# Two of four adaLN gate parts move from TensorE to VectorE in a one-core diffusion block

## The chip, the core and the metric

The kernel runs on one core of a Trainium2 chip. A core has TensorE (PE in the profile, with PEld for its weight loads), VectorE (DVE), ScalarE (ACT), GpSimd (POOL) and SyncE (SP), which here only issues DMAs. Each engine takes its instructions in the order in which they were written into its queue and waits on semaphores for the others. The metric is device time in microseconds: the median of several executions. One further execution was profiled, and all rows below are from it.

## What is computed

The reference is one layer of a diffusion block: 256 latent tokens and 256 context tokens of 2048 channels, all in fp32. The conditioning vector c gives six vectors of 2048 numbers through one matrix `w_ada`; the third of them, `g_a`, is the gate of the attention sub-layer, and it is first needed where the output projection is added to x.

```
sh_a, sc_a, g_a, sh_m, sc_m, g_m = ada_modulation(c, w_ada[layer], b_ada[layer])   # silu(c) @ w + b
h = modulate(rms_norm(x, norm_attn_w[layer]), sh_a, sc_a)
q, k, v, u = split_projection(h @ w_in[layer])
...
attn = latent_window_attention(q, k, v, kc, vc, attn_sink[layer])
pool = multiscale_pool(u, pool_w[layer], pool_scale[layer])
x = x + g_a * (jnp.concatenate([attn, pool], axis=-1) @ w_out[layer])
hm = modulate(rms_norm(x, norm_mlp_w[layer]), sh_m, sc_m)
x = x + g_m * squared_relu_mlp(hm, w_mlp_up[layer], w_mlp_down[layer])
```

## The kernel before

All weights stream through one ring. `WeightStream` holds a list of 1 MB tiles in the order of use and loads them with DMAs from the SP queue into five buffers named `raw` (`N_RAW`, L25). A load can start when the tile five places ahead in the list has been given back, and the SP queue issues the loads strictly in that order. A weight tile is split for the matmuls by ScalarE (`hi`, L97) and VectorE (`lo`, L98), and is given back after that. An adaLN tile (`in_w_ada`) is not split: it is given back when the engine that multiplies it with silu(c) has read it.

Each adaLN vector is cut into parts of 512 columns (`g` in ADA_LATE, the gate) or of 256 columns of shift and scale together (`m`). A part has four steps, one for each of its four tiles, and then a finish. There are two ways to do the steps. `ada_pe` (L292) lets TensorE multiply a step's tile with `c_sil` into `ps_ada`, four matmuls that the profile shows as eight instructions, and ScalarE copies the sum to `ada_e` after the fourth step (L311). `ada_dve` (L315) lets VectorE do it: one TENSOR_SCALAR (L325) and fifteen SCALAR_TENSOR_TENSOR (L327) for a part, four instructions for a step, each adding to the one before. In both cases a TensorE matmul over the partitions finishes the part: `ps_g` for the gate (L526), which VectorE adds to the gate tile `ga` (L528).

The list ADA_LATE (L32) fixes the order of the parts and the engine of each. `late_steps` (L514) goes through it; `run_late` (L537) does one step, and does the finish of the part before when the next part begins. During the attention 20 steps are placed: the part m1 and the four gate parts g0 to g3. The parts m2 to m4 come in the output projection (`LATE_OUT`).

The attention itself is 16 units (`Unit`, L706: eight pairs of heads by two blocks of queries). A unit is a chain over three engines: scores `ps_s` on TensorE (L717 to L720), maxima on VectorE (L728 to L730), exponentials on ScalarE (L736, L734), sum and reciprocal on VectorE (L740, L741), normalisation on ScalarE (L744), transposes `tp_p` on TensorE (L752), their copy `pT` on ScalarE (L754). After every second unit `attend` multiplies with the values (`ps_o`, L763), and ScalarE and VectorE split the result into `mx` (L766, L767). The pooling mixer (`ps_pool`) is woven in. Then comes the output projection (`ps_w`), which needs the weight tiles of `w_out`.

The order on each engine is not the written order: the kernel is built with a scheduler that lays out the program on a simulated timeline and writes each engine's queue from that. A change in one step so reorders its neighbours too. The gate parts are called part 0 to part 3 below (j in ADA_LATE).

Of the kernel before, what the change touches and what calls it, by code (L numbers as in the profile page):

```python
# [8 lines left out]
F32 = mybir.dt.float32  # L9
# [6 lines left out]
P = 128  # L16
# [14 lines left out]

ADA_LATE = (  # L32
    ("m", 0, "pe"), ("m", 1, "pe"),
    ("g", 0, "pe"), ("g", 1, "pe"), ("g", 2, "pe"), ("g", 3, "pe"),
    ("m", 2, "dve"), ("m", 3, "dve"), ("m", 4, "dve"), ("m", 5, "pe"), ("m", 6, "dve"), ("m", 7, "dve"),
)
LATE_IN = 4
# [87 lines left out]
def kernel(  # L125
# [10 lines left out]
    const = ctx.enter_context(tc.tile_pool(name="const", bufs=1, side="left"))  # L136
# [131 lines left out]
    def rstd(pool, ss, n, rest=EPS):  # L268

        nv = pool.tile([P, n], F32, tag="rs_v", name="rs_v", bufs=2)  # L270
        y = pool.tile([P, n], F32, tag="rs_y", name="rs_y", bufs=2)
        u = pool.tile([P, n], F32, tag="rs_u", name="rs_u", bufs=2)
        nc.vector.tensor_scalar(nv, ss, 1.0 / D, rest, ALU.mult, ALU.add)
        nc.vector.tensor_scalar(u.bitcast(I32), nv.bitcast(I32), 1, None, ALU.logical_shift_right)
        nc.vector.tensor_scalar(y.bitcast(I32), u.bitcast(I32), -1, 0x5F3759DF, ALU.mult, ALU.add)
        nc.vector.tensor_scalar(nv, nv, -0.5, None, ALU.mult)
        for _ in range(3):
            for c_ in range(n):
                yc, uc = y[:, c_ : c_ + 1], u[:, c_ : c_ + 1]
                nc.vector.scalar_tensor_tensor(uc, yc, nv[:, c_ : c_ + 1], yc, ALU.mult, ALU.mult)  # L280
            for c_ in range(n):
                yc, uc = y[:, c_ : c_ + 1], u[:, c_ : c_ + 1]
                nc.vector.scalar_tensor_tensor(yc, uc, 1.5, yc, ALU.add, ALU.mult)
        return y
# [30 lines left out]
    def ada_dve(finish):  # L315

        box = {}

        def step(kg):
            raw = S.next("ada")  # L320
            for j in range(4):
                sc = c_sil[:, 4 * kg + j, 0:1]
                if kg == 0 and j == 0:
                    box["e"] = mp.tile([P, 512], F32, tag="ada_v", name="ada_v", bufs=1)
                    nc.vector.tensor_scalar(box["e"], raw[:, j, :], sc, None, ALU.mult)  # L325
                else:
                    nc.vector.scalar_tensor_tensor(box["e"], raw[:, j, :], sc, box["e"], ALU.mult, ALU.add)  # L327

        return [lambda kg=kg: step(kg) for kg in range(4)] + [lambda: finish(box["e"])]

    def ada_cols(e, weights):

        ps = bank("ps_adac")
        for j in range(4):
            nc.tensor.matmul(ps[:, 2 * j : 2 * j + 2], e[:, 128 * j : 128 * j + 128], weights, start=True, stop=True)
        return ps[:, 0:8].rearrange("p (j s) -> p j s", s=2)
# [177 lines left out]
    def late_steps():  # L514
        for what, j, engine in ADA_LATE:
            ada, weights, spread = (ada_pe, sel, selb) if engine == "pe" else (ada_dve, ones[:, 0:2], ones)

            def finish(e, what=what, j=j, weights=weights, spread=spread):
                if what == "m":
                    k = slice(2 * j, 2 * j + 2)  # L520
                    ps = ada_cols(e, weights)
                    ada_scale(am[:, k], ps[:, 0:2], bcol[:, 64 + 2 * j : 66 + 2 * j], cols[:, 48 + 2 * j : 50 + 2 * j])
                    ada_shift(sm[:, k], ps[:, 2:4], bcol[:, 48 + 2 * j : 50 + 2 * j])
                else:
                    ps = bank("ps_g")
                    nc.tensor.matmul(ps, spread, e, start=True, stop=True)  # L526
                    gs = gate["a"][:, 512 * j : 512 * j + 512]
                    nc.vector.tensor_tensor(gs, ps, gs, ALU.add)  # L528

            steps = ada(finish)  # L530
            yield from steps[:4]
            late_finish.append(steps[4])
# [290 lines left out]
    mp = ctx.enter_context(tc.tile_pool(name="mp", bufs=1, side="right", reuse_waits="tile"))  # L823
# [150 lines left out]
    for b in range(7):  # L974
        acts = early[0:2] if b == 0 else [early[2], up_group()] if b == 1 else [up_group(), up_group()]
        steps = ada_dve(lambda e, b=b: gate_m_chunk(b, e)) if b < 4 else None
        for dg in range(4):
            pss = down_group(b, dg, acts)
            for i in range(2):
                accumulate(y[dg][:, i, :], pss[i], b == 0)  # L980
            if steps:
                steps[dg]()
                if dg == 3:
                    steps[4]()
# [29 lines left out]
    def finish(i, ts, last):  # L1014

        n = 3 + len(ts)
        nc.vector.tensor_reduce(mean[:, i : i + 1], ss3[:, i, 0:n], axis=AX.X, op=ALU.add)
        nc.vector.tensor_scalar(mean[:, i : i + 1], mean[:, i : i + 1], 1.0 / D, EPS, ALU.mult, ALU.add)
        ts.append(last())
        r = rstd(yp, ss3[:, i, n : n + 1], 1, mean[:, i : i + 1])  # L1020
        w = D - 1536
        for h, t in enumerate(ts):
            s = slice(1536 + w // len(ts) * h, 1536 + w // len(ts) * (h + 1))
            nc.vector.scalar_tensor_tensor(x2[:, i, s], t, r, fw[:, s], ALU.mult, ALU.mult)
        for q, eng in ((3, nc.sync), (0, nc.sync), (1, nc.scalar), (2, nc.sync)):
            xs = x2[:, i, 512 * q : 512 * q + 512]
            if q < 2 or q == 2 and i == 0:
                nc.scalar.activation(xs, xs, AF.Copy, scale=r)
            elif q == 2:
                nc.vector.tensor_scalar(xs, xs, r, None, ALU.mult)  # L1030
            eng.dma_start(out=out[P * i : P * i + P, 512 * q : 512 * q + 512], in_=xs)
# [70 lines left out]
```

## Time and profile before

| what | value |
|---|---|
| median of 3 runs | 1147.65 us (1146.72 to 1148.39) |
| the profiled execution | 1147.05 us, its span 1145.3 us |
| PE busy | 1104.6 us, 96% of the span |
| DVE busy | 779.2 us, 68% |
| ACT busy | 523.6 us, 46% |
| DMA | 286.66 MB, 250 GB/s on the mean |

The span is the profiled stretch; 1.75 us of the execution lie outside it. Busy shares are means over stages that differ: the input projection ends at about 205 us, the attention lies between about 205 and 306 us, the output projection between 306 and 402 us, and the MLP takes the rest. Matmuls overlap one another, and their ends are modelled, so a PE that is busy all the time is not at its peak.

### The profile page before, as it was taken

What the parts mean: (1) busy time and instruction counts of PE and PEld (TensorE: products, weight loads), DVE (VectorE), ACT (ScalarE), POOL (GpSimd) and SP (SyncE); (2) the same over time, 40 slices, a digit from 0 to 9 for tenths busy, and PEclk for the clock granted to TensorE, in tenths of its full rate; (3) what the DMA queues carried; (4) which work ended last, traced back from release to release, by engine and by line L of the source; (5) the groups of instructions that cost most, each with busy time, mean ns of one, the idle gap of its engine ahead of it and who ended that gap; (6) DMA issues with size and microseconds to landing.
All of it is one profiled execution on the core that took longest, in us unless ns stands there. A gap on an engine that the chain in (4) does not pass through costs nothing.

```text
span 1145.3 us, 16131 instructions
## 1 busy us (share of the span) xinstructions
PE 1104.6 (96%) x6364; PEld 909.3 (79%) x6364; DVE 779.2 (68%) x1222; ACT 523.6 (46%) x796; POOL 37.0 (3%) x53
## 2 busy tenths in 40 slices
PE   4999999999999989999999999999999999999996
PEld 2767778856588869888888888888888888888885
DVE  4655567875588988696774874884664565587576
ACT  4633233499734343365343443433444443443452
POOL 1000001610000000000000000000000000000000
PEclk9999999999999989899999999999999999999998
DMA  9999898687799989977775776775566556566532
GB/s 343 359 341 336 288 325 264 210 292 259 267 369 314 325 306 332 336 246 259 262 265 184 257 269 195 253 267 192 184 192 202 194 184 185 191 192 204 184 110 75
DMA packets 174013, 286.66 MB, mean 250 GB/s; under 512 B 5608, under 2 KB 72352, under 8 KB 172784
## 3 DMA queue, kind: packets, MB, share of 16 engines
q1 hardware_dynamic: 172800, 279.55, 72.9%
q0 software_dynamic: 848, 5.55, 1.3%
q8 instruction: 50, 0.82, 0.3%
q10 hardware_dynamic: 288, 0.52, 0.1%
q14 instruction: 27, 0.22, 0.1%
HBM read 283.50 MB, written 2.10 MB: 249 GB/s over the span
## 4 chain that ended last, share of the span: by engine, by line
PE 88%; DVE 4%; ACT 3%; DMA 3%; issue 1%; SPq 0%; ACTq 0%; DVEq 0%
PE ps_up L919 25%; PE ps_d L288 10%; PE ps_d L289 10%; PE ps_d L290 10%; PE ps_ada L305 4%; PE ps_w L288 3%; PE ps_w L290 3%; PE ps_w L289 3%; PE ps_qu L288 2%; PE ps_qu L290 2%; PE ps_qu L289 2%; PE ps_up L288 1%; DVE lo L98 1%; PE ps_o L763 1%; PE ps_up L289 1%; PE ps_up L290 1%
## 5 line engine op out<-in xcount | busy, mean ns | idle before, releaser
L98 DVE TENSOR_TENSOR lo<-raw,hi 128x1024 fp32r<-128x1024 f32 x330 | 397.7, 1226 | 211.8 <-ACT hi L97 201.0
L97 ACT CAST hi<-raw 128x1024 fp32r<-128x1024 f32 x330 | 338.1, 1050 | 409.1 <-PE ps_up L919 151.7
L919 PE MATMUL ps_up<-mx,hi 128*128 128x512 f32 x832 | 200.1, 393 | 0.0
L288 PE MATMUL ps_d<-hi,ahi 128*128 128x512 f32 (+1 forms) x520 | 200.0, 386 | 0.0
L289 PE MATMUL ps_d<-lo,ahi 128*128 128x512 f32 (+1 forms) x520 | 200.0, 386 | 0.0
L290 PE MATMUL ps_d<-hi,alo 128*128 128x512 f32 (+1 forms) x520 | 198.7, 386 | 0.0
L919 PEld LDWEIGHTS ps_up<-mx,hi 128*128 128x128 f32 x832 | 153.4, 188 | 31.8 <-issue 1.9
L290 PEld LDWEIGHTS ps_d<-hi,alo 128*128 128x128 f32 x520 | 97.7, 188 | 19.8
L288 PEld LDWEIGHTS ps_d<-hi,ahi 128*128 128x128 f32 x520 | 97.7, 188 | 19.5
L289 PEld LDWEIGHTS ps_d<-lo,ahi 128*128 128x128 f32 x520 | 97.7, 188 | 19.3
L919 PEld LDWEIGHTS ps_up<-mx,lo 128*128 128x128 f32 x832 | 106.7, 191 | 4.0
L327 DVE SCALAR_TENSOR_TENSOR ada_v<-raw,c_sil,ada_v 128x512 f32<-128x512 f32 x135 | 100.9, 748 | 12.7 <-DMA raw<-in_w_ada_dram 11.1
L919 PE MATMUL ps_up<-mx,lo 128*128 128x256 f32 x832 | 107.9, 283 | 0.0
L288 PE MATMUL ps_qu<-hhi,hi 128*128 128x256 f32 x240 | 69.3, 290 | 1.4 <-ACT hi L97 1.4
L305 PE MATMUL ps_ada<-raw,c_sil 128*32 128x512 f32 x480 | 68.3, 628 | 2.2 <-DMA raw<-in_w_ada_dram 1.9
L290 PE MATMUL ps_qu<-hhi,lo 128*128 128x256 f32 x240 | 67.0, 282 | 0.3 <-DVE lo L98 0.3
L289 PE MATMUL ps_qu<-hlo,hi 128*128 128x256 f32 x240 | 66.9, 280 | 0.0
L288 PEld LDWEIGHTS ps_qu<-hhi,hi 128*128 128x128 f32 x240 | 45.1, 188 | 16.6 <-issue 8.4
L288 PE MATMUL ps_up<-mx,hi 128*128 128x256 f32 x192 | 54.7, 293 | 1.8 <-ACT mx L884 1.5
L289 PE MATMUL ps_up<-mx,hi 128*128 128x256 f32 x192 | 54.3, 287 | 0.0
L290 PE MATMUL ps_up<-mx,lo 128*128 128x256 f32 x192 | 53.1, 287 | 0.4 <-DVE lo L98 0.4
L288 PE MATMUL ps_w<-hi,mx 128*128 128x512 f32 x128 | 50.4, 395 | 0.0
(202 smaller groups left out, 1336.4 us busy)
## 6 DMA issues: line engine op xcount, KB each, us to landing
raw<-in_w_ada_dram SPq DMA_DIRECT2D x128, 512.0 KB, 7.3
raw<-in_w_mlp_up_dram SPq DMA_DIRECT2D x64, 1024.0 KB, 5.5
raw<-in_w_mlp_down_dram SPq DMA_DIRECT2D x64, 1024.0 KB, 5.1
raw<-in_w_ada_dram SPq DMA_DIRECT2D x32, 1024.0 KB, 6.8
raw<-in_w_in_dram SPq DMA_DIRECT2D x19, 1024.0 KB, 7.6
raw<-in_w_out_dram SPq DMA_DIRECT2D x16, 1024.0 KB, 7.5
xnat<-in_x_dram SPq DMA_DIRECT2D x2, 1024.0 KB, 6.0
xnat<-in_ctx_dram SPq DMA_DIRECT2D x2, 1024.0 KB, 11.7
```

The source lines that it names most:

```text
L97: up = nc.scalar.copy(hi, raw)
L98: low = nc.vector.tensor_tensor(lo, raw, hi.bitcast(F32), ALU.subtract)
L288: nc.tensor.matmul(ps, a[0], b[0], start=first, stop=False, skip_group_check=True)
L289: nc.tensor.matmul(ps, a[0], b[1], start=False, stop=False, skip_group_check=True)
L290: nc.tensor.matmul(ps, a[1], b[0], start=False, stop=last, skip_group_check=True)
L305: nc.tensor.matmul(ps[32 * j : 32 * j + 32, :], c_sil[:, 4 * kg + j, :], raw[:, j, :], start=(kg == 0), stop=(kg == 3), tile_position=(0, ...
L327: nc.vector.scalar_tensor_tensor(box["e"], raw[:, j, :], sc, box["e"], ALU.mult, ALU.add)
L763: nc.tensor.matmul(ps[64 * i : 64 * i + 64, 0:T], va[k // 2][:, k % 2, 64 * g : 64 * g + 64], pT[:, k, i, :], start=(k == 0), stop=(k == 3 ...
L919: nc.tensor.matmul(ps, wk, h, start=part == k == 0, stop=part == 1 and k == KC - 1, skip_group_check=True)
```

## The change

In ADA_LATE the gate parts 1 and 3 change their engine from "pe" to "dve". Since the pool `mp`, from which `ada_dve` takes its tile, doesn't exist during the attention, the tile is then the one that `ada_pe` uses, `ada_e` (one buffer, in `const`).

```diff
 ADA_LATE = (
     ("m", 0, "pe"), ("m", 1, "pe"),
-    ("g", 0, "pe"), ("g", 1, "pe"), ("g", 2, "pe"), ("g", 3, "pe"),
+    ("g", 0, "pe"), ("g", 1, "dve"), ("g", 2, "pe"), ("g", 3, "dve"),
...
                 if kg == 0 and j == 0:
-                    box["e"] = mp.tile([P, 512], F32, tag="ada_v", name="ada_v", bufs=1)
+                    if mp:
+                        box["e"] = mp.tile([P, 512], F32, tag="ada_v", name="ada_v", bufs=1)
+                    else:
+                        box["e"] = const.tile([P, 512], F32, tag="ada_e", name="ada_e", bufs=1)
                     nc.vector.tensor_scalar(box["e"], raw[:, j, :], sc, None, ALU.mult)
...
+    mp = None
```

Lines behind the edit are numbered five higher in the changed kernel. The queues are the same up to the finish of part 0. From there VectorE's queue reads as follows: `ga` is the gate tile to which part 0 is added, `lo` a weight split, `st` and `ps_s` the softmax, `qs` the queries, `mx` the split result of `attend`. Before:

```order
L528 TENSOR_TENSOR ga<-ps_g,ga 128x512
L660 TENSOR_TENSOR qs_2710<-qa_273,qs_2710 64x256
L98 TENSOR_TENSOR lo<-raw,hi 128x1024
L728 TENSOR_REDUCE st<-ps_s 128x1
L98 TENSOR_TENSOR lo<-raw,hi 128x1024
L728 TENSOR_REDUCE st<-ps_s 128x1
L740 TENSOR_TENSOR st<-st 128x2
L729 SCALAR_TENSOR_TENSOR st<-st,nsink 128x2
L741 RECIPROCAL st<-st 128x2
L730 TENSOR_TENSOR st<-sink,st 128x2
```

The same place on VectorE in the changed kernel:

```order
L533 TENSOR_TENSOR ga<-ps_g,ga 128x512
L328 TENSOR_SCALAR ada_e<-raw,c_sil 128x512
L665 TENSOR_TENSOR qs_2710<-qa_273,qs_2710 64x256
L733 TENSOR_REDUCE st<-ps_s 128x1 x2
L98 TENSOR_TENSOR lo<-raw,hi 128x1024
L330 SCALAR_TENSOR_TENSOR ada_e<-raw,c_sil,ada_e 128x512
L98 TENSOR_TENSOR lo<-raw,hi 128x1024
L734 SCALAR_TENSOR_TENSOR st<-st,nsink 128x2
L745 TENSOR_TENSOR st<-st 128x2
L330 SCALAR_TENSOR_TENSOR ada_e<-raw,c_sil,ada_e 128x512
L772 TENSOR_TENSOR mx_2678<-ps_o,mx_2678 128x256
L733 TENSOR_REDUCE st<-ps_s 128x1
```

The sixteen products of part 1 now stand between the softmax rows of five units; the last of them stands three rows ahead of the addition of part 1 to `ga`, and that directly ahead of `mx` of `attend(4)`. On TensorE the finish of part 1 (`ps_g`) stands before the steps of part 2 (`ps_ada`) and `attend(4)` (`ps_o`). Before:

```order
L526 MATMUL ps_g<-ada_e,selb 128x512
L305 MATMUL ps_ada<-raw,c_sil 32x512 x16
L763 MATMUL ps_o<-pT,va_281 64x256
L752 MATMUL tp_p<-ident,p 128x128 x4
L763 MATMUL ps_o<-pT,va_281 64x256 x3
L763 MATMUL ps_o<-pT,va_282 64x256 x4
L752 MATMUL tp_p<-ident,p 128x128 x4
```

The same place on TensorE in the changed kernel:

```order
L531 MATMUL ps_g<-ada_e,ones 128x512
L305 MATMUL ps_ada<-raw,c_sil 32x512 x4
L768 MATMUL ps_o<-pT,va_281 64x256 x4
L768 MATMUL ps_o<-pT,va_282 64x256 x4
L757 MATMUL tp_p<-ident,p 128x128 x8
```

Three of the four steps of part 2 have moved behind `attend(4)`, among the scores and the pooling; the 32 matmuls of the parts 1 and 3 (64 instructions in the profile) are gone from the queue. At the end of the attention, part 3 stands on VectorE in the changed kernel, behind the addition of part 2 to `ga`; before, the products of part 3 were on TensorE, directly behind `ps_g` of part 2.

```order
L533 TENSOR_TENSOR ga<-ps_g,ga 128x512
L328 TENSOR_SCALAR ada_e<-raw,c_sil 128x512
L734 SCALAR_TENSOR_TENSOR st<-st,nsink 128x2
L330 SCALAR_TENSOR_TENSOR ada_e<-raw,c_sil,ada_e 128x512
L735 TENSOR_TENSOR st<-sink,st 128x2
L98 TENSOR_TENSOR lo<-raw,hi 128x1024
L330 SCALAR_TENSOR_TENSOR ada_e<-raw,c_sil,ada_e 128x512
L98 TENSOR_TENSOR lo<-raw,hi 128x1024
L330 SCALAR_TENSOR_TENSOR ada_e<-raw,c_sil,ada_e 128x512
L745 TENSOR_TENSOR st<-st 128x2
```

ScalarE's queue at the same end of the attention, from the exponentials of the last unit on; `hi` is the split of the second `w_out` tile. Before:

```order
L736 ACTIVATE p,st<-ps_s,st 128x512 x2
L734 ACTIVATE st<-st 128x2
L311 COPY ada_e<-ps_ada 128x512
L754 COPY pT<-tp_p 128x4x128 x2
L97 CAST hi<-raw 128x1024 x2
L744 ACTIVATE p<-p,st 128x512 x2
L766 CAST mx_3187<-ps_o 128x256
L754 COPY pT<-tp_p 128x4x128 x4
```

The same place on ScalarE in the changed kernel:

```order
L741 ACTIVATE p,st<-ps_s,st 128x512 x2
L739 ACTIVATE st<-st 128x2
L771 CAST mx_3185<-ps_o 128x256
L759 COPY pT<-tp_p 128x4x128 x2
L749 ACTIVATE p<-p,st 128x512 x2
L759 COPY pT<-tp_p 128x4x128
L97 CAST hi<-raw 128x1024 x2
L759 COPY pT<-tp_p 128x4x128
```

The split of the second `w_out` tile has moved from before the last normalisation to before the last `pT` copy, and the copies of `ada_e` for the parts 1 and 3 are gone.

## Rows read from the trace of the kernel before

**Rows 1.** The page, busy time of each engine over the span.

```profile
PE 1104.6 (96%) x6364; PEld 909.3 (79%) x6364; DVE 779.2 (68%) x1222; ACT 523.6 (46%) x796; POOL 37.0 (3%) x53
```

**Rows 2.** Windows: stretch, length, busy us of PE, PEld, DVE, ACT, POOL, clock, DMA.

```profile
235.00:255.00 20.00, 20.00 (x143) 11.70 (x143) 12.68 (x38) 18.90 (x44) 0.76 (x3) 1.00 0.75 263
255.00:275.00 20.00, 18.90 (x131) 13.21 (x131) 12.89 (x35) 18.40 (x48) 0.00 (x0) 1.00 0.76 279
279.90:294.10 14.20, 14.20 (x102) 10.83 (x99) 5.97 (x18) 11.88 (x28) 0.00 (x0) 1.00 0.73 275
294.10:306.50 12.40, 10.52 (x77) 5.03 (x75) 7.93 (x16) 11.98 (x24) 0.00 (x0) 1.00 0.78 260
306.50:402.00 95.50, 95.50 (x444) 78.07 (x445) 77.88 (x100) 38.88 (x52) 0.76 (x1) 1.00 0.99 338
```

**Rows 3.** The window of part 1, and VectorE's costliest groups in it.

```profile
253.40:280.30 26.90, 25.60 (x178) 15.18 (x176) 18.57 (x50) 25.30 (x64) 0.00 (x0) 1.00 0.69 249
...
L728 DVE TENSOR_REDUCE st<-ps_s 128x1 f32<-128x512 f32 x10 | 6.8, 686 | 5.3 <-PE ps_s L720 5.2
L98 DVE TENSOR_TENSOR lo<-raw,hi 128x1024 fp32r<-128x1024 f32 x2 | 2.4, 1221 | 0.0
```

**Rows 4.** Tile ada_v (duration min/median/max), and VectorE's timeline at 315 us.

```profile
L327 DVE SCALAR_TENSOR_TENSOR ada_v<-raw,c_sil,ada_v x135: 740/747/756, 315.8 to 762.8; 128x512 f32<-128x512 f32 x135
L325 DVE TENSOR_SCALAR ada_v<-raw,c_sil x9: 477/479/486, 311.1 to 718.6; 128x512 f32<-128x512 f32 x9
...
315.79 0.75 DVE L327 SCALAR_TENSOR_TENSOR ada_v<-raw,c_sil,ada_v 128x512 f32<-128x512 f32 x1
316.45 0.42 DVE L767 TENSOR_TENSOR mx<-ps_o,mx 128x256 fp32r<-128x256 f32 x1
```

**Rows 5.** TensorE's timeline at the finishes of parts 1 and 2: start, duration, idle before.

```profile
274.99 0.22 PE L720 MATMUL ps_s<-mask_r,ident_r 128*128 128x128 f32 x1
275.05 1.07 PE L526 MATMUL ps_g<-ada_e,selb 128*128 128x512 f32 x2
276.32 3.64 PE L305 MATMUL ps_ada<-raw,c_sil 128*32 128x512 f32 x32 [0.20 <-ACT p L736]
279.89 0.65 PE L763 MATMUL ps_o<-pT,va 128*64 128x256 f32 x2
...
294.14 1.07 PE L526 MATMUL ps_g<-ada_e,selb 128*128 128x512 f32 x2
295.14 3.64 PE L305 MATMUL ps_ada<-raw,c_sil 128*32 128x512 f32 x32
```

**Rows 6.** The chain that ended last, from part 3 to the output projection.

```profile
296.27 5.20 DMA raw<-in_w_out_dram
...
303.48 1.24 ACT p L744 x2
...
304.97 1.47 ACT pT L754 x3
...
306.48 0.65 PE ps_o L763 x2
```

**Rows 7.** ScalarE's timeline in the output projection, waits for `w_out` tiles.

```profile
313.56 1.05 ACT L97 CAST hi<-raw 128x1024 fp32r<-128x1024 f32 x1 [3.77 <-DMA raw<-in_w_out_dram]
...
322.05 2.00 ACT L97 CAST hi<-raw 128x1024 fp32r<-128x1024 f32 x2 [6.07 <-DMA raw<-in_w_out_dram]
```

**Rows 8.** Windows at the norm behind the output projection, and TensorE's timeline there.

```profile
404.00:406.00 2.00, 0.19 (x2) 0.00 (x0) 1.53 (x12) 0.81 (x3) 0.00 (x0) 1.00 1.14 399
...
408.00:410.00 2.00, 2.00 (x14) 1.33 (x17) 1.97 (x6) 1.17 (x3) 0.00 (x0) 0.50 0.09 37
...
414.00:416.00 2.00, 2.00 (x17) 0.78 (x10) 2.00 (x7) 0.00 (x0) 0.00 (x0) 0.81 0.99 362
...
407.11 0.70 PE L868 MATMUL ps_r<-diag,ones 128*128 128x256 f32 x2 [2.92 <-DVE diag L866]
...
409.00 6.49 PE L305 MATMUL ps_ada<-raw,c_sil 128*32 128x512 f32 x32
```

## Prediction

> **What bounds the kernel now.** I read the page first: TensorE is busy 96% of the span and VectorE 68% [rows 1], so by the means the change moves work from the fuller engine to the emptier one. But it touches one stage only, so next come windows of that stage [rows 2]. In the attention (235 to 295 us) three engines are near their limit together: TensorE 18.9 to 20.0 of 20 us, ScalarE 18.4 to 18.9, while VectorE has 12.7 to 12.9. The end of the attention (294.1 to 306.5) is different: TensorE has 1.9 us of idle there, and ScalarE is busy 12.0 of 12.4. The output projection behind it keeps TensorE busy for all of 95.5 us and the DMA engines 0.99. So a microsecond by which the output projection starts later is not won back there, and the question is when it starts: now with the `ps_o` of the last head pair at 306.48 [rows 6].
>
> Third is the window of part 1, from the addition of part 0 to the gate at 253.4 to the reciprocals at 280.3, where VectorE is busy 18.57 of 26.9 us with 50 instructions; 5.3 us of its idle time lie ahead of the maxima, which wait for TensorE's scores [rows 3]. Fourth, TensorE's timeline: `ps_g` of part 1 at 275.05, the four steps of part 2 in one burst of 3.64, `attend(4)` at 279.89, `ps_g` of part 2 at 294.14, then the burst of part 3 [rows 5]. Between 279.9 and 294.1 TensorE has no idle time [rows 2]. Last, the chain at the end: a `w_out` load of 5.20 us that starts when part 3 gives its first tile back, a last normalisation, three copies, `ps_o` [rows 6].
>
> **The change, part by part.** *Removed from TensorE:* eight steps. Four take 3.64 us in a burst [rows 5], 0.91 each, so 7.3 us. *Removed from ScalarE:* two copies to `ada_e`. *Added to VectorE:* two times one TENSOR_SCALAR of 0.48 us and fifteen SCALAR_TENSOR_TENSOR of 0.747 us [rows 4]. Each depends on the one before, but where another instruction stands between, the next starts 0.66 us later (315.79 to 316.45 [rows 4]); this is the lower price. A part is 10.3 us at 0.66 (15 x 0.66 + 0.4) and 11.7 at 0.747. SP's queue keeps its order; what changes is when a tile is given back and so when the load five places on starts.
>
> *Part 1.* Its products now stand between the softmax rows, and the matmul `ps_g` of part 1 waits for the last one. VectorE must do, from 253.4 on, what it did there (18.57, less 0.6 for the addition of part 1, which comes behind `ps_g`, so 18.0) and 10.3 more: 28.3 us, to 281.7, if it never waits. In that window it now idles 8.3 us, and the new work fills just that. I take 281.7. Bounds: 280.7 if overlaps of neighbouring instructions save another microsecond; 284.5 with 0.747 a product (11.7 in place of 10.3) and 1.4 us of waits left. TensorE has nothing else in its queue to do: the scores ahead of `ps_g` end at 275 as now, or 276 where the split of their queries on VectorE stands behind products of part 1, and behind it stand one step of part 2 and `attend(4)`. So that starts at 281.7 + 0.95 (`ps_g`) + 0.91 = 283.6 and not at 279.89: **+3.7 us** (+2.7 to +6.5). The four steps that TensorE no longer does here turn into its wait. Behind the waiting `ps_g` stand the transposes, the pooling and the scores of all later units; ScalarE waits for these.
>
> *Part 2.* Three of its four steps no longer lie ahead of `attend(4)` but in the stretch up to `ps_g` of part 2, in which TensorE had no idle time [rows 2]: 3 x 0.91 = **+2.7 us** (0 to +2.7). The Trainium skill, Perfetto Trace Analysis, "Identifying the Most-Contended Engine", says that matmul busy time is a bad measure of how full TensorE is and that weight-load busy time is the better one. By it TensorE has room in that stretch, PEld being busy 10.83 of 14.2 us [rows 2], the three steps would fit in, and the sum would be 2.7 us less. I follow PE's row, since the order in the queue is fixed and no instruction there waits.
>
> *Part 3 and the end of the attention.* Now 306.48 - 294.14 = 12.3 us pass from `ps_g` of part 2 to the last `ps_o`. The burst of part 3 leaves TensorE, but the chain there runs over the load of the second `w_out` tile, and that starts when the first tile of part 3 is given back, now after 0.91 us of TensorE. In the changed kernel VectorE has to do ahead of that, behind `ps_g`: the addition to the gate (0.7, as a row of 128x512 [rows 3]), 0.48, three products of 0.66, two `lo` of 1.2 [rows 3] and two small rows, 0.3: 5.9 us. With `ps_g` (0.95) the load starts 6.8 us behind the start of `ps_g` and lands, at 5.20 us, at 12.0. The two casts (2.00 [rows 7]) stand ahead of the last `pT` copy (0.5, a third of 1.47 [rows 6]): 14.5 us, so **+2.2 us**. If the tile is given back early enough, what is left is the chain without it: maxima, exponentials, `attend(6)`, normalisation and copies end at about 11.9 us, -0.4; if the first `w_out` tile is late as well, whose `lo` stands ahead, +4.
>
> *TensorE's clock.* Behind the output projection TensorE now waits for the norm: 0.19 us busy in 404 to 406 and a wait of 2.92 us. From 408 on the granted clock is 0.50, which is 1.2 of 2.4 GHz, and it is back only after 414; four adaLN steps take 6.49 us there and not 3.64 [rows 5, 8]. That is 2.85 us, and 0.5 for the first microsecond at half speed: 3.3 us for such a wait. The wait for `ps_g` of part 1 would be 281.7 - 276 = 5.7 us, longer than that, and the work behind it stands on the path: **+3.3 us**. Ends: 0, if the clock stays, and 6.6, if it also falls at the end of the attention, where TensorE waits some 4 us for the `w_out` tile. The Trainium skill, TensorE: Matmul & The Clock Gate, "HAM oscillation — how this bites in real kernels", states that a stalled TensorE is throttled and starts its next batch at half rate, which speaks against any change that makes it wait; the rows agree, with 0.50.
>
> *Output projection.* Part 3's later tiles are given back over some 20 us and no longer within 3.6, and the loads of the `w_out` tiles queue behind them. ScalarE now waits 3.77 and 6.07 us for tiles in that stretch [rows 7], without TensorE waiting; of this slack some is used up. I take **+1.0 us** (0 to +4).
>
> Sum: 3.7 + 2.7 + 2.2 + 3.3 + 1.0 = 12.9 us. The profiled execution took 1147.05 (span 1145.3 and 1.75 outside); 1147.05 + 12.9 = 1159.95, and the median of the runs lies 0.6 above the profiled one: **1160.5 us**. About 0.2%, 2.3 us, is what a measurement can tell from no change.
>
> **The rivals.**
> 1. *TensorE is the bound and VectorE has room* (the other side). If VectorE is through with part 1 in time, the 7.3 us of TensorE are won, and the end is 1147.65 - 7.3 = 1140.4. For it: 96% against 68% [rows 1], TensorE full in the attention [rows 2]. Against it: 8.3 us of idle time for 10.3 us of work [rows 3, 4]. What decides is the start of `ps_g` of part 1: with the three steps at their price and the end of the attention unchanged, the change breaks even where 1.86 + 2.7 behind `ps_g` gives 279.89, at 275.3. Only ahead of that is there a gain.
> 2. *VectorE late, but the clock stays.* Without the clock's term: 1157.2. For it: no wait in the attention has lowered the clock so far (1.00 in all windows [rows 2]). Against it: none of them came near 5 us.
> 3. *Two falls of the clock and late tiles.* With 6.6 for the clock and 4 for the tiles: 1160.5 + 3.3 + 3.0 = 1166.8. For it: 0.99 of the DMA engines in use behind [rows 2], tiles held by VectorE. Against it: the fall of the clock at the start of the projection gives the tiles time.
> 4. *It comes out even.* VectorE's wait falls on what TensorE saves: 1147.65, with `ps_g` of part 1 at about 275.
>
> **How the numbers follow.** Forecast 0.45, rival 2 0.25, rival 3 0.14, rival 4 0.08, rival 1 0.08. So faster by over 0.2% 0.08, within 0.2% 0.08, slower 0.84. The range goes from 1150, which is rival 2 with the low ends of part 1 (-1.0), part 2 (-2.7), the end of the attention (-2.6) and the tiles (-1.0), 1149.9, to 1168, just above rival 3; outside lie rivals 1 and 4 and some of rival 3, 0.2 in all.
>
> **What would show it.** Right: VectorE busy nearly all of 254 to 281; `ps_g` of part 1 near 281.7, with an idle time of over 4 us on TensorE ahead of it that is put down to `ada_e` on VectorE; a granted clock of 0.50 for some microseconds behind it; `ps_g` of part 2 some 9 us later than 294.14; the last `ps_o` waiting for `pT` behind a split of a `w_out` tile, near 318. It would be wrong if VectorE finishes part 1 before 277, if no row of TensorE waits for `ada_e`, or if the output projection starts later and the end doesn't move.

## The result, and the profile after

The changed kernel takes 1159.34 us (median of 4 executions, 1158.41 to 1161.97), the kernel before on the same chip 1148.02. The ratio, an estimate over the executions and not the quotient of the two medians, is 1.0104, with an interval of 1.0084 to 1.0125: 1% slower. The forecast was 1160.5 us, in a range of 1150 to 1168. The profiled execution took 1158.42 us, its span is 1156.6, 11.3 us longer than that of before.

The page gives the same picture by its means as in [rows 1], TensorE 95%, VectorE now 69%; but TensorE's clock has a new dent, in the slice from 260 to 289 us, where the attention lies. Two lines of the changed kernel's page, busy time and granted clock in 40 slices:

```profile
PE 1103.6 (95%) x6300; PEld 911.4 (79%) x6300; DVE 800.9 (69%) x1254; ACT 523.9 (45%) x794; POOL 35.9 (3%) x53
...
PEclk9999999997999989999999999999999999999999
```

64 instructions have left TensorE, and it is busy for only 1.0 us less, since others take longer at the lower clock, as `ps_g` of part 1 below with 2.07 us for 1.07 [rows 5]. VectorE has 32 instructions more. So the next view is the stage. TensorE's timeline of the changed kernel (start, duration, idle time before and who ended it):

```profile
256.86 0.65 PE L768 MATMUL ps_o<-pT,va 128*64 128x256 f32 x2 [1.29 <-ACT pT L759]
...
264.74 1.54 PE L757 MATMUL tp_p<-ident,p 128*128 128x128 f32 x6 [3.04 <-ACT p L749]
...
284.82 2.07 PE L531 MATMUL ps_g<-ada_e,ones 128*128 128x512 f32 x2 [6.23 <-DVE ada_e L330]
286.82 1.51 PE L305 MATMUL ps_ada<-raw,c_sil 128*32 128x512 f32 x8
288.27 1.08 PE L768 MATMUL ps_o<-pT,va 128*64 128x256 f32 x8
...
305.39 1.07 PE L531 MATMUL ps_g<-ada_e,selb 128*128 128x512 f32 x2
...
314.37 1.67 PE L757 MATMUL tp_p<-ident,p 128*128 128x128 f32 x8 [2.47 <-ACT p L749]
315.97 1.11 PE L768 MATMUL ps_o<-pT,va 128*64 128x256 f32 x2
...
322.93 1.94 PE L768 MATMUL ps_o<-pT,va 128*64 128x256 f32 x14
```

The 6.23 us ahead of `ps_g` of part 1, put down to `ada_e` on VectorE, are the wait that was forecast. The 3.04 us ahead of `tp_p` were not. Windows of the changed kernel (length, busy us of PE, PEld, DVE, ACT, POOL, granted clock, DMA share and GB/s):

```profile
253.40:284.00 30.60, 20.85 (x123) 16.32 (x120) 28.16 (x67) 25.79 (x62) 0.00 (x0) 0.84 0.58 198
...
262.00:264.00 2.00, 0.00 (x0) 0.00 (x0) 2.00 (x7) 1.95 (x8) 0.00 (x0) 0.97 0.67 173
264.00:266.00 2.00, 1.26 (x6) 1.27 (x7) 1.91 (x6) 1.41 (x4) 0.00 (x0) 0.50 1.05 383
...
282.00:284.00 2.00, 0.00 (x0) 0.00 (x0) 2.00 (x8) 1.19 (x5) 0.00 (x0) 0.50 0.14 54
284.00:286.00 2.00, 1.18 (x2) 0.50 (x2) 1.00 (x5) 2.00 (x6) 0.00 (x0) 0.50 0.08 19
...
316.00:318.00 2.00, 2.00 (x5) 1.09 (x5) 1.58 (x3) 1.33 (x2) 0.00 (x0) 0.50 1.10 363
```

VectorE is busy for 28.16 of 30.6 us, where it had 8.3 us of idle time [rows 3]. TensorE stands still in 262 to 264 and in 280 to 284, and behind each of these, and behind the wait at 314, the clock is at 0.50.

Four more starts are needed for a table by stage: the addition of part 0 to `ga`, and the MLP's first `ps_up`, each before and after.

```profile
253.39 0.69 DVE L528 TENSOR_TENSOR ga<-ps_g,ga 128x512 f32<-128x512 f32 x1
255.66 0.68 DVE L533 TENSOR_TENSOR ga<-ps_g,ga 128x512 f32<-128x512 f32 x1
...
415.41 0.50 PE L288 MATMUL ps_up<-mx,hi 128*128 128x256 f32 x2
426.05 0.50 PE L288 MATMUL ps_up<-mx,hi 128*128 128x256 f32 x2
```

With these, the rows above and those ahead of the prediction:

| from, to | before, us | after, us | difference | forecast |
|---|---|---|---|---|
| start, `ga` of part 0 | 253.39 | 255.66 | +2.3 | 0 |
| `ga` of part 0, `ps_o` of `attend(4)` | 26.50 | 32.61 | +6.1 | +3.7 and 3.3 for the clock |
| `attend(4)`, `ps_g` of part 2 | 14.25 | 17.12 | +2.9 | +2.7 |
| `ps_g` of part 2, the last head pair's first `ps_o` | 12.34 | 10.58 | -1.8 | +2.2 |
| that `ps_o`, `ps_up` | 108.93 | 110.08 | +1.2 | +1.0 |
| `ps_up`, end | 729.89 | 730.55 | +0.7 | 0 |
| span | 1145.3 | 1156.6 | +11.3 | +12.9 |

The order of the instructions doesn't explain the first line: up to `ga` of part 0 the queues are the same, in this kernel and in all those below, and in their 13 profiled executions that addition starts anywhere between 252.60 and 255.66 us. In this execution the clock fell to 0.65 in 236 to 238 behind a wait of 1.89 us for `pT`; before, behind 1.76 us at the same place, it stayed at 1.00.

### The profile page after: what moved, and what is told of

It reads as the page before. It is cut to its first block, busy times and chain, and to the rows that moved or that the text cites. A ratio compares the mean times of both kernels' runs of the same rounds, so it can differ in the third digit from the quotient of the medians.

```text
span 1156.6 us, 16029 instructions
## 1 busy us (share of the span) xinstructions
PE 1103.6 (95%) x6300; PEld 911.4 (79%) x6300; DVE 800.9 (69%) x1254; ACT 523.9 (45%) x794; POOL 35.9 (3%) x53
## 4 chain that ended last, share of the span: by engine, by line
PE 81%; DVE 7%; DMA 6%; ACT 4%; issue 1%; SPq 0%; POOL 0%; ACTq 0%; DVEq 0%
PE ps_up L924 25%; PE ps_d L290 10%; PE ps_d L289 10%; PE ps_d L288 10%; PE ps_ada L305 4%; DMA raw<-in_w_mlp_up_dram 3%; PE ps_w L288 3%; PE ps_w L289 3%; PE ps_w L290 3%; DVE lo L98 2%; PE ps_qu L288 2%; PE ps_qu L290 2%; PE ps_qu L289 2%; PE ps_o L768 1%; DMA raw<-in_w_ada_dram 1%
## 5 line engine op out<-in xcount | busy, mean ns | idle before, releaser
L330 DVE SCALAR_TENSOR_TENSOR ada_v<-raw,c_sil,ada_v 128x512 f32<-128x512 f32 x135 | 100.8, 747 | 14.5 <-DMA raw<-in_w_ada_dram 13.1
L305 PE MATMUL ps_ada<-raw,c_sil 128*32 128x512 f32 x416 | 62.1, 636 | 1.1 <-DMA raw<-in_w_ada_dram 1.1
L290 PE MATMUL ps_up<-mx,lo 128*128 128x256 f32 x192 | 53.2, 285 | 0.5 <-DVE lo L98 0.5
L289 PE MATMUL ps_w<-lo,mx 128*128 128x512 f32 x128 | 50.5, 395 | 0.0
```

Of the source, the lines that this page charges most:

```text
L289: nc.tensor.matmul(ps, a[0], b[1], start=False, stop=False, skip_group_check=True)
L290: nc.tensor.matmul(ps, a[1], b[0], start=False, stop=last, skip_group_check=True)
L305: nc.tensor.matmul(ps[32 * j : 32 * j + 32, :], c_sil[:, 4 * kg + j, :], raw[:, j, :], start=(kg == 0), stop=(kg == 3), tile_position=(0, ...
```

## The experiments

Each kernel was timed beside runs of the kernel before on the same chip; the medians of before lay between 1146.81 and 1147.44 us there. A ratio is to those runs. The edits shown are against the changed kernel, except where the text says otherwise, and are cut to the lines around the change.

### Each part alone

```diff
-    ("g", 0, "pe"), ("g", 1, "dve"), ("g", 2, "pe"), ("g", 3, "dve"),
+    ("g", 0, "pe"), ("g", 1, "dve"), ("g", 2, "pe"), ("g", 3, "pe"),
```
```diff
-    ("g", 0, "pe"), ("g", 1, "dve"), ("g", 2, "pe"), ("g", 3, "dve"),
+    ("g", 0, "pe"), ("g", 1, "pe"), ("g", 2, "pe"), ("g", 3, "dve"),
```

The first is `g1_only`, the second `g3_only`.

> Only part 1 goes to VectorE; part 3 stays on TensorE as before. Theory (the loss is part 1's wait on TensorE, and part 3 gives a little back): nearly the whole loss of 11 us, and 1.8 us more since part 3 no longer shortens the end of the attention: 1158 to 1162 us; the matmul ps_g of part 1 waits 5 to 7 us. Rival (the loss is in part 3, whose tiles VectorE holds, and in the late w_out tiles): 1146 to 1150 us.

> Only part 3 goes to VectorE; part 1 stays on TensorE as before. Theory (part 3 costs nothing, its four steps leave TensorE at the end of the attention): 1144 to 1149 us, the last ps_o up to 1.8 us nearer to ps_g of part 2 than before. Rival (part 3's tiles are given back late and the w_out tiles with them): 1156 to 1160 us, with ps_o or ps_w waiting for a split of a w_out tile.

Part 1 alone: 1155.31 us, ratio 1.0067 (1.0051 to 1.0083). Part 3 alone: 1152.07, ratio 1.0046 (1.0031 to 1.0060). Each lies between the ranges of its theory and its rival, and by these totals both parts cost. Only in the attention, and only beside part 1, does part 3 give something back: from `ga` of part 0 to the last pair's first `ps_o` it takes 53.1 us before, 62.4 with part 1 alone, 60.3 with both and 54.1 with part 3 alone (table under "Part 2 instead"). With part 1 alone the wait for `ada_e` is the same 6.23 us. With part 3 alone, ScalarE's and TensorE's timelines at the end of the attention:

```profile
303.36 1.33 ACT L749 ACTIVATE p<-p,st 128x512 f32<-128x512 f32 x2 [1.90 <-DVE st L746]
304.60 0.35 ACT L771 CAST mx<-ps_o 128x256 fp32r<-128x256 f32 x1
304.85 1.07 ACT L759 COPY pT<-tp_p 128x512 f32<-128x512 f32 x2
305.81 2.00 ACT L97 CAST hi<-raw 128x1024 fp32r<-128x1024 f32 x2
307.70 1.09 ACT L759 COPY pT<-tp_p 128x512 f32<-128x512 f32 x2
```
```profile
308.35 1.11 PE L768 MATMUL ps_o<-pT,va 128*64 128x256 f32 x2 [2.95 <-ACT pT L759]
```

Here is what the prediction expected of the changed kernel itself: the last `pT` copies stand behind the split of a `w_out` tile, and `ps_o` waits for them. The normalisation too is late, by 1.90 us: VectorE's small softmax rows stand behind three products. From `ps_g` of part 2 (295.00) to this `ps_o` it is 13.35 us, 1.0 more than before, and the clock is at 0.50 from 308 to 312.

### The finish of part 1 later

```diff
-            yield from steps[:4]
-            late_finish.append(steps[4])
+            yield from steps[:3]
+            if what == "g" and j == 2:
+                late_finish.append(held.pop())
+            yield steps[3]
+            if what == "g" and j == 1:
+                held.append(steps[4])
+            else:
+                late_finish.append(steps[4])
...
+    held = []
```

`late_finish` has this with both parts on VectorE, `late_g1` with part 1 alone.

> Both parts on VectorE as in the change, but the finish of part 1 is asked for three steps later, so that TensorE's queue has the steps of part 2 and the ps_o of two units ahead of its ps_g. Theory (TensorE loses because it stands waiting at ps_g, and the clock falls behind that wait): those 4 + 3 us and the 2.7 of the displaced steps come back, 1147 to 1152 us. Rival (VectorE's load delays the softmax rows themselves, wherever ps_g stands): at most 2 us come back, 1157 to 1160 us, and TensorE then waits for transposes (tp_p) or scores instead.

> Only part 1 on VectorE and its finish asked for three steps later, as in the run with the late finish; part 3 on TensorE. Theory (the two costs add: the late finish takes away part 1's wait, part 3's cost of 5 us is a matter of its own): 1146 to 1149 us. Rival (part 1's load on VectorE costs 5 us wherever its finish stands, and part 3 costs little next to it): 1151 to 1154 us.

With both parts on VectorE 1152.98 us, ratio 1.0051 (1.0032 to 1.0069): just over the theory's 1152, well under the rival's 1157. Asking for one matmul later, around which the scheduler lays out the queues anew, takes away about half of the loss. TensorE's waits in 205 to 330 (waited for, us in total, times, longest):

```profile
PE ps_o L775 <- ACT pT L766: 6.6, 4, 2.6
PE tp_p L764 <- ACT p L756: 3.0, 1, 3.0
PE ps_g L531 <- DVE st L740: 1.6, 1, 1.6
```

The wait for `ada_e` is gone. With part 1 alone on VectorE and the later finish it is 1150.19 us, ratio 1.0024 (1.0009 to 1.0038), between the two expectations: of part 1's 0.67% some 0.43 go with the wait, and a quarter of a per cent stays. The traces don't show where that quarter lies: the profiled execution of `late_g1` is the fastest of its nine, 3.5 us below their median, and that of `late_finish` the fastest of eight, 3.4 us below. The wait of 3.0 us at `tp_p` is in both kernels.

### What taking the work off TensorE is worth

```diff
-            for j in range(4):
+            for j in range(4 if mp else 2):
```
```diff
-            for j in range(4):
+            for j in range(4 if mp else 1):
+                if kg and not mp:
+                    break
```

During the attention `mp` is None, so the edits touch the parts 1 and 3 alone: the first, `half_products`, leaves out the last two of the four products of each step; the second, `no_products`, leaves out all sixteen of a part but the first.

> Leaves out the last two of the four products of each step of the parts 1 and 3 on VectorE (8 products a part instead of 16), everything else as in the change. Theory (VectorE's time is what lacks: 10.3 us of new work for 8.3 us of idle time): with 5 us the work fits, ps_g of part 1 waits under 1 us and the time is 1142 to 1148 us. Rival (the new order and the wait between the engines cost, not VectorE's load): 1154 to 1160 us.

> Leaves out the products of the parts 1 and 3 but the first of each part: neither TensorE nor VectorE does them (VectorE's 30 SCALAR_TENSOR_TENSOR are gone, TensorE's eight steps too). What is measured is the worth of taking the eight steps off TensorE. Theory formed after the first runs (the steps of part 1 stood in TensorE's wait for the softmax, so that their removal only opens a gap of some 3 us and a fall of the clock there): 1142 to 1148 us, at most 5 us won, with a tp_p that waits some 3 us near 262. Rival (the removal is worth its 7.3 us, and VectorE's load alone eats it in the other runs): 1138 to 1141 us, no such wait.

Half the products: 1146.24 us, ratio 0.9990 (0.9975 to 1.0005), `ps_g` of part 1 without a wait. That is in the theory's range, but a kernel with eight steps less on TensorE and only half of them on VectorE is no faster than before. In the attention, VectorE's halved work leaves 1.8 us of the 7.2 by which the changed kernel is longer there (54.9 and 60.3 us, for 53.1 before). No products at all: 1150.0, ratio 1.0016 (1.0003 to 1.0028), above both expectations. Leaving the work out altogether wins nothing, in the attention either (54.7 us), so the rival, which gives the removal 7.3 us, falls. Why, TensorE's timeline of the kernel before shows, at the steps of part 1 (L305), and then of the kernel without products:

```profile
252.08 1.06 PE L305 MATMUL ps_ada<-raw,c_sil 128*32 128x512 f32 x8
...
253.80 1.06 PE L305 MATMUL ps_ada<-raw,c_sil 128*32 128x512 f32 x8
...
255.52 1.06 PE L305 MATMUL ps_ada<-raw,c_sil 128*32 128x512 f32 x8
256.52 0.65 PE L763 MATMUL ps_o<-pT,va 128*64 128x256 f32 x2
...
261.23 1.06 PE L305 MATMUL ps_ada<-raw,c_sil 128*32 128x512 f32 x8
262.23 1.09 PE L752 MATMUL tp_p<-ident,p 128*128 128x128 f32 x8
```
```profile
255.92 0.65 PE L770 MATMUL ps_o<-pT,va 128*64 128x256 f32 x2 [1.29 <-ACT pT L761]
263.23 1.27 PE L759 MATMUL tp_p<-ident,p 128*128 128x128 f32 x8 [2.47 <-ACT p L751]
...
301.86 1.12 PE L770 MATMUL ps_o<-pT,va 128*64 128x256 f32 x2 [3.42 <-ACT pT L761]
```

The steps stood among the scores, ahead of matmuls that need ScalarE's results. Without them TensorE comes to these sooner and waits. In the kernel before `tp_p` (262.23) starts 8.84 us after `ga` of part 0, in the changed kernel (264.74) 9.08 us after it, without any of the four steps and with 3.04 us of idle time.

### The work left on TensorE as well

```diff
             raw = S.next("ada")
+            if not mp:
+                if kg == 0:
+                    box["ps"] = bank("ps_ada")
+                for j in range(4):
+                    nc.tensor.matmul(
+                        box["ps"][32 * j : 32 * j + 32, :], c_sil[:, 4 * kg + j, :], raw[:, j, :],
+                        start=(kg == 0), stop=(kg == 3), tile_position=(0, 32 * j),
+                    )
```

`both_engines` has this with both parts on VectorE, `both_g3` with part 3 alone, `both_late` with both parts and the later finish of part 1.

> The changed kernel, but TensorE also still multiplies the tiles of the parts 1 and 3, into a sum that nobody reads. Nothing is left out. Theory (taking part 1's steps off TensorE wins nothing since they stood in its waits; VectorE's load is the cost): 1156 to 1161 us, like the changed kernel, no fall of the clock near 264, and ps_g of part 1 still waits 5 us or more. Rival (the removal is worth its 7.3 us): 1164 to 1168 us.

> Part 3 alone on VectorE, but TensorE also still multiplies its tiles, into a sum that nobody reads. Theory (part 3's cost of 5 us is TensorE's emptied queue at the end of the attention: a wait of 2.95 us for the last pT copies and the fall of the clock behind it): 1147 to 1149 us, no fall of the clock between 300 and 320. Rival (part 3's cost is VectorE's: tiles given back late, small softmax rows behind products): 1151 to 1154 us, and a wait for the last pT copies as without the dead work.

> Both parts on VectorE, the finish of part 1 asked for three steps later, and TensorE still multiplies the tiles of both parts, into a sum that nobody reads. Nothing is left out; VectorE's load is that of the changed kernel. Theory (VectorE's load costs nothing by itself; the loss is TensorE's: its wait at ps_g, its emptied queue, and the falls of the clock behind these): 1146 to 1150 us, no wait over 1 us at tp_p near 262 or at ps_g of part 1. Rival (VectorE's load delays the softmax rows themselves): 1152 to 1156 us.

`both_engines`: 1155.73 us, ratio 1.0065 (1.0049 to 1.0080). The changed kernel with eight steps of dead work more on TensorE is not slower than the changed kernel but 0.4% faster, just under the theory's 1156. TensorE's timeline, and its windows:

```profile
262.75 1.07 PE L325 MATMUL ps_ada<-raw,c_sil 128*32 128x512 f32 x8
264.15 1.27 PE L765 MATMUL tp_p<-ident,p 128*128 128x128 f32 x8 [0.34 <-ACT p L757]
...
282.47 2.05 PE L539 MATMUL ps_g<-ada_e,ones 128*128 128x512 f32 x2 [5.97 <-DVE ada_e L338]
```
```profile
264.00:266.00 2.00, 1.85 (x12) 1.57 (x13) 1.97 (x5) 1.95 (x7) 0.00 (x0) 1.00 1.05 383
...
280.00:282.00 2.00, 0.00 (x0) 0.00 (x0) 2.00 (x8) 1.89 (x7) 0.00 (x0) 0.50 0.05 17
```

As expected, `tp_p` waits 0.34 us and not 3.04, the clock stays at 1.00 there, and the wait for `ada_e` and the fall of the clock behind it are as in the changed kernel. So the steps do cover the wait at `tp_p`, but the attention is no shorter for it, 60.3 us in both, since `ps_g` waits for VectorE either way. The 4.3 us by which this span is shorter lie elsewhere: 0.8 ahead of the change, 1.1 in the projection, 2.4 in the MLP.

`both_g3`: 1146.38 us, ratio 0.9997 (0.9986 to 1.0007); by the total the dead work takes away all of part 3's 0.46%, just under the theory's 1147. But not in the way expected: `ps_o` still waits 3.31 us for `pT` behind a split, as the rival had it, and the clock is at 0.61 and 0.53 from 310 to 314. Its `ps_up` starts at 420.3, as late as with part 3 alone (420.8); the 5 us are won in the MLP, behind that (below), and the attention is no shorter than with part 3 alone (54.6 and 54.1 us). `both_late`: 1151.66, ratio 1.0027 (1.0015 to 1.0039), between both expectations. So some 0.3% stay where neither the finish nor the emptied queue is at work: there `ps_o` waits 2.79 us for `pT` at the end of the attention, as with part 3 alone, and the normalisation ahead of it waits 1.65 us for VectorE's reciprocal. That VectorE's load delays softmax rows, the rival, is therefore not excluded for this rest.

### Part 2 instead

```diff
-    ("g", 0, "pe"), ("g", 1, "dve"), ("g", 2, "pe"), ("g", 3, "dve"),
+    ("g", 0, "pe"), ("g", 1, "pe"), ("g", 2, "dve"), ("g", 3, "pe"),
```

> Only part 2 goes to VectorE, parts 1 and 3 on TensorE. In its stretch (276 to 294) TensorE has no idle time and VectorE some 9 us of it for 10.3 us of work. Theory (what counts is whether VectorE is through before TensorE's queue comes to ps_g, and whether the steps removed were work and not cover): within 3 us of the kernel before, 1145 to 1150 us, with a wait for ada_e under 3 us. Rival (any part on VectorE costs 5 us or more in the attention): 1152 to 1156 us.

1147.69 us, ratio 1.0003 (0.9994 to 1.0013): the theory's time, but not by its reason. The wait for VectorE ahead of `ps_g`, expected under 3 us, is as long as with part 1, and the clock falls behind it:

```profile
298.86 2.05 PE L531 MATMUL ps_g<-ada_e,ones 128*128 128x512 f32 x2 [6.24 <-DVE st L745]
...
480.98 0.98 PE L288 MATMUL ps_up<-mx,hi 128*128 128x256 f32 x6 [0.46 <-ACT mx L889]
```

`ps_up` starts at 421.2, 5.8 us later than before, and the end is as before. The other row shows where that is made good. The kernel before, same place of the MLP, timeline and a window:

```profile
475.44 1.13 PE L335 MATMUL ps_adac<-ones,ada_v 128*128 128x2 f32 x8 [0.67 <-DVE ada_v L327]
478.08 1.65 PE L288 MATMUL ps_up<-mx,hi 128*128 128x256 f32 x6 [1.51 <-ACT mx L884]
```
```profile
478.00:480.00 2.00, 1.92 (x9) 1.92 (x10) 1.23 (x3) 0.43 (x2) 0.00 (x0) 0.50 1.05 387
```

There the MLP waits for an adaLN part of VectorE (`ada_v`) and for `mx`, and the clock falls; with part 2 on VectorE it does not. All profiled executions by stage: where `ga` of part 0 starts, the attention from there to the last pair's first `ps_o`, the projection from that to `ps_up`, the MLP from `ps_up` to the end, and the clock between 474 and 494 us:

| kernel | `ga` at | attention, us | projection, us | MLP, us | clock in the MLP |
|---|---|---|---|---|---|
| before | 253.4 | 53.1 | 108.9 | 729.9 | falls |
| changed | 255.7 | 60.3 | 110.1 | 730.5 | falls |
| g1_only | 254.1 | 62.4 | 109.0 | 727.6 | falls |
| g3_only | 254.3 | 54.1 | 112.4 | 729.7 | falls |
| late_finish | 254.7 | 52.4 | 114.2 | 726.4 | stays |
| late_g1 | 252.6 | 54.0 | 108.7 | 729.7 | falls |
| half_products | 255.0 | 54.9 | 111.7 | 724.5 | stays |
| no_products | 254.7 | 54.7 | 110.2 | 727.5 | falls |
| both_engines | 254.9 | 60.3 | 109.0 | 728.1 | falls |
| both_g3 | 255.1 | 54.6 | 110.5 | 724.4 | stays |
| both_late | 254.9 | 55.3 | 110.6 | 729.9 | falls |
| g2_only | 254.8 | 57.7 | 108.8 | 724.6 | stays |
| norm_cover (next section) | 253.0 | 53.2 | 105.7 | 727.8 | stays |

The MLP is shorter where the clock stays, but the groups touch (727.5 and 727.8). The attention tells the parts apart better than the totals do. Part 2 alone costs 4.6 us there, which its MLP gives back. The later finish takes away nearly all that the attention lost: 60.3 becomes 52.4, and with part 1 alone 62.4 becomes 54.0, though these two are the fastest executions of their kernels. What `late_finish` still loses in this execution stands in the projection, where TensorE waits 3.9 us for `x` on VectorE and not 1.1. Each row is one execution, but before and norm_cover, whose edit lies behind the attention, agree in it to 0.1 us.

### Dead work in a wait of the kernel before

The edit is against the kernel before.

```diff
     transpose_group(3)
+    for _ in range(3):
+        nc.tensor.matmul(bank("ps_c"), ones, x2[:, 1, 3 * 512 : 4 * 512], start=True, stop=True)
```

> The kernel before with three matmuls more, of 128x512, whose result nobody reads, in TensorE's wait for the norm behind the output projection (2.92 us). Theory (a fall of the clock behind a wait of about 3 us costs some 3 us, and dead work in the wait prevents it): 0 to 1 us for ps_r that starts later, 3 us won by the clock, so 1144 to 1146 us, granted clock 1.00 from 408 to 416. Rival (the fall costs nothing in the end, since the MLP's first tiles are what is waited for, or the clock falls all the same): 1147 to 1149 us.

1141.51 us, ratio 0.9960 (0.9946 to 0.9975): faster than the kernel before, and more than expected. TensorE's timeline, and two windows:

```profile
403.73 2.74 PE L861 MATMUL ps_c<-x,ones 128*128 128x512 f32 x6
406.91 0.67 PE L870 MATMUL ps_r<-diag,ones 128*128 128x256 f32 x2 [0.44 <-DVE diag L868]
...
408.30 3.64 PE L305 MATMUL ps_ada<-raw,c_sil 128*32 128x512 f32 x32
```
```profile
408.00:410.00 2.00, 2.00 (x20) 0.82 (x23) 1.96 (x8) 1.40 (x4) 0.00 (x0) 1.00 0.52 214
...
478.00:480.00 2.00, 2.00 (x19) 2.00 (x18) 1.93 (x3) 0.26 (x1) 0.00 (x0) 1.00 1.06 389
```

The wait is 0.44 us in place of 2.92, the four steps behind take 3.64 in place of 6.49 [rows 8], and `ps_up` starts at 411.87, 3.5 us earlier, of which 0.4 lie ahead of the attention. Another 2.1 us come from the MLP (727.8 in place of 729.9), where the clock now stays at 1.00 too.

## Why the prediction was right, and where not

**Part 1, right.** VectorE had no room. `ps_g` was to start 28.3 us after `ga` of part 0 and did so 29.2 after it; the wait was to be 5.7 us and is 6.23; the clock behind it falls to 0.50. With the clock's effect on `ps_g` (2.07 for 1.07) and the step (1.51 for 1.06), 1.45 us, taken out of the +6.1, the term of +3.7 measured 4.7. That the wait is the cost in the attention, and not the products as such, the later finish shows: with VectorE's work the same, 0.5% of 1.0% come back, and in the profiled execution all that the attention had lost (52.4 us, for 60.3 in the changed kernel and 53.1 before).

**The removed steps, right in the sum, for a reason that was half seen.** The prediction let TensorE's 7.3 us turn into the wait at `ps_g`. They turned into waits sooner: the steps were cover for ScalarE's and VectorE's part of the softmax, and without them a wait of 3.04 us and a fall of the clock stand at 264. That rival 1 was wrong does not hang on VectorE's room alone: without any products nothing is won either, by the time or in the attention.

**Part 2, right.** +2.9 for +2.7. The Trainium skill, Perfetto Trace Analysis, "Identifying the Most-Contended Engine", by which the three steps would have fitted in at no cost, did not hold here: PE's row, full in that stretch [rows 2], was the one to follow.

**Part 3 and the end of the attention, wrong.** The step was "the two casts stand ahead of the last `pT` copy: 14.5 us, so +2.2 us". It measured 10.58, -1.8, below even the low end that the prediction gave (-0.4). ScalarE's order was read rightly, the consumer was not: the first `ps_o` of the last pair needs the first head's copy (315.06), which stands ahead of the split (316.67); only the other copy (318.57) stands behind it, and its `ps_o` comes at 322.93, with `ps_w` in between. ScalarE's timeline of the changed kernel there:

```profile
315.06 0.59 ACT L759 COPY pT<-tp_p 128x512 f32<-128x512 f32 x1
316.67 1.99 ACT L97 CAST hi<-raw 128x1024 fp32r<-128x1024 f32 x2 [1.02 <-DMA raw<-in_w_out_dram]
318.57 0.58 ACT L759 COPY pT<-tp_p 128x512 f32<-128x512 f32 x1
```

Where part 1 isn't late as well (part 3 alone), the step holds, with +1.0.

**The clock, right in kind, short in number.** One fall was counted, 3.3 us. The changed kernel has three in the attention behind the change, at 264, 282 and 316. The one that was counted, at 282, cost 1.45 us on `ps_g` and the step and not 3.3: the clock had fallen within the wait, and from 288 it is at 1.00 again. The second fall of rival 3, at the end of the attention, came too, behind a wait for `p`, but without its price: the projection is 1.2 us longer. The Trainium skill, TensorE: Matmul & The Clock Gate, "HAM oscillation — how this bites in real kernels", has a stalled TensorE throttled; the rows agree, with 0.50 behind each of these waits. In the kernel before, one such fall at the norm is worth 0.4%, measured by taking it away, with the one in the MLP that went with it.

**"A microsecond by which the output projection starts later is not won back there", too narrow.** It holds for the projection (+1.2), but the MLP behind it can give back up to 5 us, as with part 2 alone. In the changed kernel it gave nothing back (730.5).

The total came out close in part by luck, since the errors had opposite signs: the end of the attention 4 us too high, and 2.3 us ahead of the change that no step had. Without these 2.3 us, which the queues don't explain, the span would be 9.0 us longer and not 11.3.

What stays open: why the first tiles of the MLP come out in one of the two ways. In the eight executions in which the clock falls, TensorE waits 0.56 to 1.47 us for `ada_v` and 1.51 for `mx`; in four of the five in which it stays, it waits 0.46 to 0.49 us for `mx` alone. But `late_finish` has both waits, 0.36 and 1.51 us, and the clock stays, so whether `ada_v` is ready isn't all of it. Which late load or split decides it no run tells apart, and differences under some 5 us between the times of two of these kernels can't be assigned to the attention alone for this reason. Nor is it shown what the 2.3 us ahead of the change are, or that they are in every execution.

## What to carry to other kernels

Here work that stood ahead of an instruction which would have waited anyway cost nothing where it was, and taking it off the fullest engine won nothing; look at what the instruction behind it waits for, not at the engine's busy share. Before an in-order engine is made to wait for a slower chain, ask whether its consumer can stand later in the queue: here that was worth half of the loss. Where the times of two kernels differ by little, compare the stage that was changed too: here other stages moved by as much. And three dead matmuls in a wait of 2.92 us on TensorE were worth 0.4%, more than the wait.

## What the runs showed of the hardware

Waits of the same length at the same place, behind the same queue, ended in a fall of the clock in one execution and not in another. At `ps_o` near 235 us a wait of 1.89 us was followed by 0.65 in the changed kernel, one of 1.91 and one of 1.92 us by 1.00 with part 1 and with part 3 alone; 2.65 us there were followed by 0.50 with half the products, with none, and in `both_g3`, and by 1.00 in `both_engines` and with part 2 alone. The 22 waits of 2.91 to 6.24 us between 205 and 420 us, in all executions together, were each followed by 0.50.
